# Input halves padded to 320 columns at one address modulo 256, and weight rings one buffer shorter, in an mLSTM and HGRN2 step

## The chip, the core and the metric

The kernel runs on one core of a Trainium2 chip. The metric is the device time of one execution in microseconds. A core has TensorE (PE, with the loading of weights shown apart as PEld), VectorE (DVE), ScalarE (ACT), GpSimd (POOL) and SyncE (SP, which issues the DMAs). Each engine works through its own rows in a fixed order and waits on semaphores for the others.

## What is computed

The reference is one step of a streaming encoder layer: 512 prompt columns of a new stream and 32 sample columns of a running one, D = 1024. In float32:

```python
xn = _rmsnorm(h, norm_g[l])
proj = xn @ w_in[l]
u, v_m, z_m, ig_pre, fg_pre, q_h, f_h, i_h, g_h, ga, gb = jnp.split(proj, _split_points(), axis=-1)
c, conv_new = _causal_conv(u, conv0[l].astype(u.dtype), conv_w[l], conv_b[l])
c = jax.nn.silu(c).astype(f32)
...
hm, C_new, n_new, m_new = _mlstm(qm, km, vm, ig, lf, C0[l].astype(f32), n0[l].astype(f32), m0[l].astype(f32))
hm = _head_layernorm(hm.transpose(0, 2, 1, 3), mnorm_g[l].astype(f32))
hm = (hm + m_skip[l].astype(f32) * c) * jax.nn.silu(z_m.astype(f32))
ya = hm.astype(x.dtype) @ w_brm[l]
...
oh, S_new = _hgrn(to_heads(qh), to_heads(kh), to_heads(i_h.astype(f32)), to_heads(lfh), S0[l].astype(f32))
oh = _head_rmsnorm(oh.transpose(0, 2, 1, 3), hnorm_g[l].astype(f32)) * jax.nn.silu(g_h.astype(f32))
yb = oh.astype(x.dtype) @ w_brh[l]
y = jax.nn.sigmoid(ga) * ya + jax.nn.sigmoid(gb) * yb
h = h + y @ w_out[l]
h = h + jax.nn.sigmoid(h @ w_pg[l]) * (p[l] @ w_ple[l])
```

`_mlstm` has 4 heads of width 512 (q and k are projections of the convolved u, with a causal convolution of width 4), `_hgrn` has 8 heads of width 128. The outputs are the normalised h and the new states.

## The kernel before

All activations lie with channels on the 128 partitions and the T = 544 columns (32 sample, 512 prompt) along the free axis; D is 8 such tiles. A matmul's output is one half, TH = 272 columns.

To keep float32 accuracy every projection is made of rounded parts: a value x is split into a high part (rounded to the matmul type, by ACT) and a low part (the rest, by DVE), and three matmuls add up high by high, high by low and low by high. The normalised input is kept for the whole kernel in `xs`: eight pairs `xh`, `xl` of 128x544 tiles (`norm`, `norm_low`, L1438 to 1447). Three functions read it as the moving operand: `dense` (L199; v of head 0, f = 1 to 3), `One` (L431; z of head 0) and `Two` (L549; all other projections). `Two` forms two output tiles out of seven products of half size instead of eight. A block is one product: 12 matmuls of 272 columns with one weight piece of 128x512. Its forms a11, a12 and s4 read a half of `xh`/`xl` (`moving`, L533), the forms s2, s3, s1 and a22 read one of the four slices of `xfh`/`xfl`, which are sums and differences of halves (`xf_sums`). The same class with another `xs` (the tiles `yh`, `yl`) makes `w_out`.

Weights pass through rings in SBUF, which all have buffers of 128 x 512 fp32:

- "wr": the raw piece, written by a DMA on SP (`raw_piece`), NRAW = 6 buffers
- "wh" and "wl": its high part, written by ACT, and its low part, by DVE (`split_piece` at L174 and L175, `high_piece`, `low_piece`), NPIECE = 6 buffers each
- "wu": sums of raw pieces for the forms s1 to s4 (`add`, L482), NSUM = 4 buffers

A buffer can be written again when the last row that reads it is done. For "wr" these readers are the split and the sums; for "wh" and "wl" they are PE's matmuls of the block.

What sets the order: PE's rows stand in an order written by hand throughout. ACT's and DVE's do so up to about 65 us and in the HGRN2 chain; in the heads of the mLSTM (about 50 to 650 us) and at the end, a scheduler places the rows when their inputs and buffers are free by its own estimate. `Pump` puts the blocks in order and calls for the splits AHEAD = 3 blocks ahead. Whatever order comes out is fixed in the program.

Other names that are spoken of: L904 and L906 copy transposed gate columns (`col`, `cols`) out of PSUM; `emc` (L1202, L1203) are small copies of them; L988 and L989 make high and low parts of q; L573 and L577 put projections of u into the convolution's input `ub`; L774 is a step of the convolution (`cv`); L1280 and L1282 scale y ahead of its transposes (L1290); L138 makes low parts of the merged head (`hm`); `wbm..` are weights of the merge `ya`.

## Time and profile before

| | |
|---|---|
| median of 3 runs | 1118.29 us (1117.81 to 1118.54) |
| span of the profiled execution | 1116.3 us |
| PE busy | 1108.7 us (99%), 8825 rows |
| DVE busy | 922.1 us (83%), 1969 rows |
| ACT busy | 714.8 us (64%), 1583 rows |
| granted TensorE clock | 1.00 in every stage |
| DMA, mean of the span | 122 GB/s |

The span is the time from the first to the last instruction of the execution that the profiler recorded; the time of a run has some more around it. A busy share counts time in which an engine works on at least one row; PE's matmuls overlap, so the time of a row (0.29 us for 272 columns) is longer than the pitch from one start to the next. Pitches are therefore taken from start times.

### The profile page before, as it was taken

What the parts mean: (1) busy time and instruction counts of PE and PEld (TensorE: products, weight loads), DVE (VectorE), ACT (ScalarE), POOL (GpSimd) and SP (SyncE); (2) the same over time, 40 slices, a digit from 0 to 9 for tenths busy, and PEclk for the clock granted to TensorE, in tenths of its full rate; (3) what the DMA queues carried; (4) which work ended last, traced back from release to release, by engine and by line L of the source; (5) the groups of instructions that cost most, each with busy time, mean ns of one, the idle gap of its engine ahead of it and who ended that gap; (6) DMA issues with size and microseconds to landing.
All of it is one profiled execution on the core that took longest, in us unless ns stands there. A gap on an engine that the chain in (4) does not pass through costs nothing.

```text
span 1116.3 us, 23756 instructions
## 1 busy us (share of the span) xinstructions
PE 1108.7 (99%) x8825; PEld 1097.3 (98%) x8825; DVE 922.1 (83%) x1969; ACT 714.8 (64%) x1583; POOL 158.4 (14%) x412
## 2 busy tenths in 40 slices
PE   9999999999999999999999999999999999999998
PEld 9999999999999999999999999999999999999998
DVE  6986998676896786986898699999999888789785
ACT  6686657754666555664667478787777776445662
POOL 5112021101010110101200123222322000000000
PEclk9999999999999999999999999999999999999999
DMA  6234225232264132461556322122222353333943
GB/s 224 77 95 128 86 67 176 96 114 96 74 215 157 39 124 104 131 222 53 195 176 206 107 77 83 56 84 74 84 75 74 109 166 114 111 125 103 304 150 119
DMA packets 78044, 135.78 MB, mean 122 GB/s; under 512 B 8804, under 2 KB 16612, under 8 KB 77928
## 3 DMA queue, kind: packets, MB, share of 16 engines
q1 hardware_dynamic: 77760, 134.21, 36.9%
q8 instruction: 69, 1.13, 0.4%
q14 instruction: 47, 0.39, 0.1%
q10 hardware_dynamic: 168, 0.06, 0.0%
HBM read 109.32 MB, written 24.91 MB: 120 GB/s over the span
## 4 chain that ended last, share of the span: by engine, by line
PE 94%; DVE 3%; ACT 1%; DMA 1%; issue 1%; SPq 0%; ACTq 0%; DVEq 0%
PE d L549 42%; PE ya L199 9%; PE pg L2017 4%; PE yb L199 4%; PE k L199 4%; PE q L199 4%; PE C L1069 3%; PE pl L1741 3%; PE u L326 2%; PE sc L1012 2%; PE v L199 2%; PE nm L1248 2%; PE d L431 1%; PE ple L199 1%; PE yt L1290 1%; PE ho L1855 1%
## 5 line engine op out<-in xcount | busy, mean ns | idle before, releaser
L566 ACT COPY t<-d 128x272 f32<-128x272 f32 x126 | 47.4, 376 | 5.2 <-PE d L549 5.0
L1762 DVE TENSOR_TENSOR hkq<-hkq,hq 128x288 f32<-128x288 f32 (+1 forms) x96 | 41.5, 439 | 5.6 <-PE pl L1741 2.5
L1696 ACT COPY km<-hkq 128x256 f32<-128x256 f32 x56 | 23.9, 427 | 30.5 <-DVE hkq L1762 28.4
L1741 PE MATMUL pl<-hkq,km 128*128 128x128 f32 x224 | 37.9, 291 | 0.6 <-ACT km L1696 0.6
L774 DVE SCALAR_TENSOR_TENSOR cv<-ub,vec,cv 128x547 f32<-128x547 f32 x48 | 37.0, 781 | 0.4
L1741 PEld LDWEIGHTS pl<-hkq,km 128*128 128x128 f32 x224 | 30.9, 190 | 2.7 <-ACT km L1696 1.6
L1177 DVE SCALAR_TENSOR_TENSOR c<-c,wi,Cs 128x258 f32<-128x258 f32 x32 | 15.1, 477 | 20.2 <-PE Cs L1175 20.1
L1081 ACT COPY Co<-C 128x258 f32<-128x258 f32 x30 | 9.8, 379 | 28.3 <-PE C L1069 20.7
L1316 DVE TENSOR_TENSOR y<-ya,y 128x272 f32<-128x272 f32 x48 | 18.8, 432 | 8.8 <-PE ya L199 8.7
L1776 DVE COPY_PREDICATED at<-lmask,pl 128x256 f32<-128x256 uint8 (+1 forms) x56 | 25.3, 452 | 0.3
L1259 ACT COPY y<-nm 128x516 f32<-128x516 f32 x16 | 9.4, 589 | 18.0 <-PE nm L1248 17.8
L1026 ACT CAST sh<-dm 128x512 fp32r<-128x512 f32 (+3 forms) x16 | 7.4, 459 | 20.4 <-DVE dm L1020 20.4
L939 POOL COPY vsm<-vt 128x96 f32<-128x96 f32 x16 | 7.2, 462 | 87.4 <-ACT vt L577 44.3
L1069 PE MATMUL C<-vh,kwh 128*128 128x258 f32 x96 | 19.3, 283 | 0.0
L1069 PE MATMUL C<-vh,kwl 128*128 128x258 f32 x96 | 19.3, 282 | 0.0
L1069 PE MATMUL C<-vl,kwh 128*128 128x258 f32 x96 | 19.3, 282 | 0.0
L1012 PE MATMUL sc<-q,kh 128*128 128x512 f32 (+3 forms) x80 | 18.6, 320 | 0.1
L1207 DVE BATCH_NORM_STATS2 bs<-y 128x6 f32<-128x512 f32 (+1 forms) x20 | 13.7, 687 | 5.1 <-ACT y L1259 5.0
L963 DVE TENSOR_TENSOR kl<-kf,kh 128x512 fp32r<-128x512 f32 x16 | 11.0, 686 | 8.1 <-ACT kh L962 8.0
L767 POOL COPY uo<-ub 128x3 f32<-128x3 f32 x16 | 7.6, 472 | 64.1 <-DVE ub L573 39.3
L1248 PE MATMUL nm<-vh,sh 128*128 128x258 f32 x80 | 16.5, 288 | 0.0
L1768 POOL TENSOR_TENSOR hq<-hq 128x136 f32<-128x136 f32 (+4 forms) x40 | 16.0, 399 | 3.1
(4666 smaller groups left out, 5119.2 us busy)
## 6 DMA issues: line engine op xcount, KB each, us to landing
ya_d<-y SPq DMA_DIRECT2D x32, 272.0 KB, 3.0
y<-ya_d SPq DMA_DIRECT2D x24, 272.0 KB, 3.8
c<-in_C SPq DMA_DIRECT2D x16, 258.0 KB, 4.5
out_Cs<-c SPq DMA_DIRECT2D x16, 258.0 KB, 2.8
out_Cp<-Co SPq DMA_DIRECT2D x15, 258.0 KB, 2.4
x<-in_xT SPq DMA_DIRECT2D x8, 272.5 KB, 4.7
ya<-ya_d SPq DMA_DIRECT2D x8, 272.0 KB, 4.8
h<-in_xT SPq DMA_DIRECT2D x8, 272.0 KB, 2.8
```

The source lines that it names most:

```text
L199: PE.matmul(both[b][:m, :TH], part(w, off + k * step, m, x), xx[:, half(b)], start=(k == 0 and j == 0), stop=(k == n - 1 and j == 2),)
L549: PE.matmul(ps, ww[:, c], xx, start=(start and k == 0 and j == 0), stop=end, skip_group_check=not start,)
L566: S.copy(t, ps)
L774: last = V.scalar_tensor_tensor(cv[:, :547], ub[:, j : j + 547], vcol(V_CW + 4 * ft + j), cv[:, :547], ALU.mult, ALU.add)
L1012: PE.matmul(pn[:, 0, :n], ks[f][x][:, j * P : (j + 1) * P], qs[f][y][:, NS + j * P : T], start=(f == 0 and i == 0), stop=(f == KH - 1 and ...
L1069: PE.matmul(pn[g][:, :VH], kw[b][x][:, f * P : (f + 1) * P], vv[b][y][:, g * VH : (g + 1) * VH], start=(b == 0 and j == 0), stop=(b == NB ...
L1248: PE.matmul(pn[:, g, :VH], st[j][x][:, (i - j) * P : (i - j + 1) * P], vv[j][y][:, g * VH : (g + 1) * VH], start=(j == 0 and q == 0), stop ...
L1696: S.copy(km.rearrange("p (n j c) -> p n j c", j=2, c=c), view(kk, HB, ((2 * c, NA // (2 * c)), (c - HB, 2), (1, c))),)
L1741: PE.matmul(pn[:, b * P : (b + 1) * P], km[:, b * P : (b + 1) * P], view(qq, b * P, ((2 * c, P // (2 * c)), (HB + c, 2), (1, c))), start=True,
L1762: V.tensor_tensor(x, x, t, ALU.mult)
L1776: V.copy_predicated(at[:, :n], lmask[:, li, :n], pn[:, :n])
L2017: PE.matmul(ps, part(w, k * P, P, x), xx[:, c], start=(k == 0 and j == 0), stop=(k == KD - 1 and j == 2))
```

## The change

Each tile of `xs` (and the tiles `yh`, `yl`) becomes 2 x 320 columns, of which each half uses the first 272. Two tiles that nothing uses (`gap`, 24 and 40 columns) move what follows them. All three piece rings lose a buffer: 16 tiles x 2 x 48 columns x 4 bytes are 6144 bytes a partition, as three buffers of 2048. Six small tiles have one buffer instead of two. `One` loses its parameter `cut`, which was always T/2 (TH).

```diff
+TW = 320
...
-NRAW = 6
+NRAW = 5
 NSUM = 4
-NPIECE = 6
+NPIECE = 5
...
+    gp = ctx.enter_context(tc.tile_pool(name="gp", bufs=1))
...
+    gp.tile([P, 24], F32, name="gap")
...
+    def xhalf(t, b):
+        return t[:, b * TW : b * TW + TH] if t.shape[-1] == 2 * TW else t[:, half(b)]
+
+    def xall(t):
+        return two(t)[:, :, :TH]
...
-                        xx[:, half(b)],
+                        xhalf(xx, b),
...
-        V.tensor_tensor(u, h1, l1, ALU.add)
+        V.tensor_tensor(two(u), xall(h1), xall(l1), ALU.add)
         for b, t in enumerate((x21, x22)):
-            V.tensor_tensor(t, h2[:, half(b)], l2[:, half(b)], ALU.add)
+            V.tensor_tensor(t, xhalf(h2, b), xhalf(l2, b), ALU.add)
...
-                        for b, c in enumerate(halves):
+                        for b in range(2):
                             PE.matmul(
-                                self.ps[b][:, : c.stop - c.start],
+                                self.ps[b][:, :TH],
                                 part(self.w, k * P, P, x),
-                                xx[:, c],
+                                xhalf(xx, b),
...
-                return tuple(x[:, b * TH : (b + 1) * TH] for x in self.xs[i * (KD // 2) + k])
+                return tuple(xhalf(x, b) for x in self.xs[i * (KD // 2) + k])
...
-            xh = cp.tile([P, T], F32R, name=f"xh{k}")
-            xl = cp.tile([P, T], F32R, name=f"xl{k}")
-            S.copy(xh, t[:, :T])
+            xh = cp.tile([P, 2 * TW], F32R, name=f"xh{k}")
+            xl = cp.tile([P, 2 * TW], F32R, name=f"xl{k}")
+            S.copy(xall(xh), two(t[:, :T]))
             xs.append((xh, xl))
...
-            V.tensor_tensor(xs[k][1], xt[k][:, :T], xs[k][0].bitcast(F32), ALU.subtract)
-
+            V.tensor_tensor(xall(xs[k][1]), two(xt[k][:, :T]), xall(xs[k][0].bitcast(F32)), ALU.subtract)
+
+        cp.tile([P, 40], F32, name="gap")
...
-            c = one if f == k else slice(0, T)
-            S.copy(yh[:, c], t[:, c])
-            V.tensor_tensor(yl[:, c], t[:, c], yh[:, c].bitcast(F32), ALU.subtract)
+            n = 1 if f == k else 2
+            yh, yl, tt = xall(yh)[:, :n], xall(yl)[:, :n], two(t[:, :T])[:, :n]
+            S.copy(yh, tt)
+            V.tensor_tensor(yl, tt, yh.bitcast(F32), ALU.subtract)
```

The number of rows on each engine and PE's order stay as they are. The scheduler's order of ACT and DVE differs in many places. Two of them are shown. A row gives the line, the operation, output from inputs and the shape; lines after the change are 8 or 9 higher.

DVE in q of head 0, before (`wq010l`, `wq011l` are low parts of q's weights for PE's next tile, `kl` and `q_` low parts of k and q):

```order
L963 TENSOR_TENSOR kl_1235<-kf_1200,kh_1234 128x512
L175 TENSOR_TENSOR wq010l<-wq01r_1391,wq010h 128x512
L175 TENSOR_TENSOR wq011l<-wq01r_1393,wq011h 128x512
L904 COPY col<-cols 128x72
L906 COPY cols<-cols 96x12
L989 TENSOR_TENSOR q_1330<-q_1305,q_1330 128x272
L989 TENSOR_TENSOR q_1330<-q_1304,q_1330 128x272
```

DVE at the same place after the change:

```order
L971 TENSOR_TENSOR kl_1240<-kf_1205,kh_1239 128x512
L912 COPY col<-cols 128x72
L914 COPY cols<-cols 96x12
L1210 COPY emc<-col 128x4 x2
L1211 COPY emc<-cols 32x1 x2
L997 TENSOR_TENSOR q_1303<-q_1277,q_1303 128x272
L997 TENSOR_TENSOR q_1335<-q_1310,q_1335 128x272
L997 TENSOR_TENSOR q_1335<-q_1309,q_1335 128x272
L184 TENSOR_TENSOR wq010l<-wq01r_1396,wq010h 128x512
L184 TENSOR_TENSOR wq011l<-wq01r_1398,wq011h 128x512
```

The two low parts of weights have moved behind the column copies, four `emc` copies and three low parts of q.

DVE in the projection of u of head 1, before (`wa..` and `ws..` are weight pieces of plain and summed forms; the L482 row is the sum that `ws310` is made from):

```order
L175 TENSOR_TENSOR wa1210l<-wi10r_4464,wa1210h 128x512
L482 TENSOR_TENSOR ws_4643<-wi10r_4371,wi11r_4373 128x512
L138 TENSOR_TENSOR hm7l<-c_2856,hm7h 128x544
L573 TENSOR_TENSOR ub_4385<-d_4384,t_4462 128x272
L175 TENSOR_TENSOR ws310l<-ws_4643,ws310h 128x512
L175 TENSOR_TENSOR ws110l<-ws_4576,ws110h 128x512
L573 TENSOR_TENSOR ub_4586<-d_4585,t_4604 128x32
L573 TENSOR_TENSOR ub_4586<-d_4585,t_4604 128x240
L774 SCALAR_TENSOR_TENSOR cv_4682<-ub_4385,vec,cv_4682 128x547
```

DVE at the same place after the change:

```order
L184 TENSOR_TENSOR wa1210l<-wi10r_4469,wa1210h 128x512
L147 TENSOR_TENSOR hm7l<-c_2861,hm7h 128x544
L490 TENSOR_TENSOR ws_4632<-ws_4583,wi10r_4469 128x512
L581 TENSOR_TENSOR ub_4390<-d_4389,t_4467 128x272
L490 TENSOR_TENSOR ws_4648<-wi10r_4376,wi11r_4378 128x512
L581 TENSOR_TENSOR ub_4591<-d_4590,t_4609 128x32
L581 TENSOR_TENSOR ub_4591<-d_4590,t_4609 128x240
L782 SCALAR_TENSOR_TENSOR cv_4687<-ub_4390,vec,cv_4687 128x547
L184 TENSOR_TENSOR ws310l<-ws_4648,ws310h 128x512
L184 TENSOR_TENSOR ws110l<-ws_4581,ws110h 128x512
```

The sum for `ws310` has moved behind the first `ub` row, and the low parts of `ws310` and `ws110` behind the second pair of `ub` rows and the convolution step. Head 2 has the same rows with other numbers.

## The prediction

> **What bounds the kernel now.** I read the busy shares first, then the chain that ended last, then the list of who waited for whom on PE, and then the order of time on PE and DVE around the places where the change moves rows.

> ```profile
> span 1116.3 us, 23756 instructions
> PE 1108.7 (99%) x8825; PEld 1097.3 (98%) x8825; DVE 922.1 (83%) x1969; ACT 714.8 (64%) x1583; POOL 158.4 (14%) x412
> PE 94%; DVE 3%; ACT 1%; DMA 1%; issue 1%; SPq 0%; ACTq 0%; DVEq 0%
> PE d L549 42%; PE ya L199 9%; PE pg L2017 4%; PE yb L199 4%; PE k L199 4%; PE q L199 4%; PE C L1069 3%; PE pl L1741 3%; PE u L326 2%; PE sc L1012 2%; PE v L199 2%; PE nm L1248 2%; PE d L431 1%; PE ple L199 1%; PE yt L1290 1%; PE ho L1855 1%
> ```

> PE is busy in 99% of the span and carries 94% of the chain, and 42% of the chain is one line, the matmuls of `Two` (L549). DVE at 83% and ACT at 64% have room on average. The longest total that the wait list gives for any line of PE is:

> ```profile
> PE warm L1386 <- DVE emc L1201: 1.1, 1, 1.1
> ```

> So PE hardly ever waits. Two things follow. Whatever changes the pitch of PE's matmuls counts in full. And any weight that DVE or ACT delivers later than PE wants it is a new wait that counts in full too, because there is no other wait that could swallow it. The change does one thing of each kind. The span is 1116.3 us and the median of the runs 1118.29, so about 2.0 us lie around the span; I add and subtract on the span and put these 2.0 us back. A measurement of this kernel can tell about 0.2% (2.2 us) from no change; so "same" is 1116.05 to 1120.53.

> **First part: the address of the moving operand.** A half of 272 fp32 columns is 1088 bytes, 64 more than a multiple of 256. By the program's allocations the halves of `xh` now start at 0 and 64 modulo 256 and those of `xl` at 128 and 192; with 320 columns and the two gap tiles all four start at 160. The four slices of `xfh`/`xfl` (sums of halves, also 272 columns) start at 160, 224, 32 and 96, and stay. So the trace of before already has matmuls with the moving operand at 160: the blocks of form s2 (weights `ws2..`). Here are starts of four blocks of 12 matmuls that follow each other without a break (columns: start, duration, engine, line, operation, output from inputs):

> ```profile
> 458.50 0.29 PE L549 MATMUL d<-xfh,wa2212h 128*128 128x272 f32 x1
> ...
> 460.02 0.29 PE L549 MATMUL d<-xfh,ws214h 128*128 128x272 f32 x1
> ...
> 461.50 0.29 PE L549 MATMUL d<-xh,ws412h 128*128 128x272 f32 x1
> ...
> 463.01 0.29 PE L549 MATMUL d<-xh,wa1214h 128*128 128x272 f32 x1
> ```

> The durations are alike, so they tell nothing; the pitch does. The block at 96 takes 460.02 - 458.50 = 1.52 us, the one at 160 takes 1.48, the first on `xh`/`xl` (64, 192) 1.51. Over the whole trace I averaged the pitch in all such blocks of 12: 33 at 160 give 123.8 ns a matmul, 129 blocks on `xh`/`xl` give 125.6, the other `xf` slices 125.5 (224), 126.3 (32) and 126.5 (96). The first and the last undisturbed block at 160:

> ```profile
> 231.15 0.29 PE L549 MATMUL d<-xfh,ws220h 128*128 128x272 f32 x1
> ...
> 232.50 0.29 PE L549 MATMUL d<-xfh,ws220l 128*128 128x272 f32 x1
> ...
> 936.86 0.29 PE L549 MATMUL d<-xfh,ws294h 128*128 128x272 f32 x1
> ...
> 938.22 0.29 PE L549 MATMUL d<-xfh,ws294l 128*128 128x272 f32 x1
> ...
> 938.34 0.29 PE L549 MATMUL d<-xh,ws486h 128*128 128x272 f32 x1
> ...
> 939.85 0.29 PE L549 MATMUL d<-xh,wa1294h 128*128 128x272 f32 x1
> ```

> Eleven pitches: 1.35 and 1.36 us, 123 to 124 ns each; the block on `xh`/`xl` right behind the last one takes 939.85 - 938.34 = 1.51, 126 ns each. The plain forms of L549 (1656 matmuls), z of head 0 at L431 (192) and three of the v tiles of head 0 at L199 (144) read `xh`/`xl`: 1992 matmuls move to 160. The block means price that at 1.8 ns x 1992 = 3.6 us; the mean of every 272-column matmul by its own address (124.2 at 160 against 125.3 to 126.2 at 0, 64, 128 and 192) prices it at about 1.4 x 1992 = 2.8. The address is not the only thing that differs between the blocks, so I take the middle, 1.6 ns: **-3.2 us**, bounds -2.7 and -3.6.

> [...]

> The same edit turns ACT's and DVE's writes of `xh`, `xl`, `yh`, `yl` and the sums from 128x544 into 2x272. The element count is the same:

> ```profile
> L1447 DVE TENSOR_TENSOR xl<-x,xh x8: 714/716/727, 35.2 to 43.3; 128x544 fp32r<-128x544 f32 x8
> ...
> 44.24 0.42 PE L199 MATMUL v<-xh,wv10h 128*128 128x272 f32 x2
> ```

> The eighth is done at 44.0. PE's projection of v reads the first tile from 44.2 and the eighth 42 matmuls, some 5 us, later: nothing; if a 2x272 row took twice as long, the eighth would come 5 us later and PE would wait a few tenths.

> **Second part: one buffer less in the rings.** Counts stay. What moves is order: a split of a weight piece can be placed only when a buffer of `wh` and `wl` is free, which is now one block of 12 later, and ACT and DVE run in a fixed order. Rows of DVE and ACT change at some 250 and 300 places. Mostly a piece had been ready 7 to 9 us ahead of PE and is now ready 6 us ahead: nothing. It matters where the piece falls behind something that itself waits; these are five places.

> Site A, q of head 0:

> ```profile
> 86.16 0.68 DVE L175 TENSOR_TENSOR wq010l<-wq01r,wq010h 128x512 fp32r<-128x512 f32 x1
> 87.89 0.52 PE L199 MATMUL q<-cs0h,wq010h 128*128 128x272 f32 x2
> 88.00 0.23 DVE L904 COPY col<-cols 128x72 f32<-128x72 f32 x1 [0.56 <-PE cols L902]
> 88.15 0.16 DVE L906 COPY cols<-cols 96x12 f32<-96x12 f32 x1
> 88.23 0.78 DVE L989 TENSOR_TENSOR q<-q,q 128x272 fp32r<-128x272 f32 x2
> 88.49 0.41 PE L199 MATMUL q<-cs0h,wq010l 128*128 128x272 f32 x2
> 90.29 0.16 DVE L1202 COPY emc<-col 128x4 f32<-128x4 f32 x1
> 90.36 0.14 DVE L1203 COPY emc<-cols 32x1 f32<-32x1 f32 x1
> ```

> Now `wq010l` is made at 86.16, ahead of the copy `col`, which waits for PE's transposes until 88.00. After the change DVE does `col` (0.15 from start to start), `cols` (0.08), four small copies `emc` (0.07 each), three low parts of q (0.39 each), and only then `wq010l` (0.68): 88.00 + 0.15 + 0.08 + 0.28 + 1.17 + 0.68 = 90.36. PE wants it at 88.49: **+1.9**. (ACT's high part, wanted at 87.89, is some 0.7 late too and lies inside the 1.9.) Behind `wq010l` stand `wq011l`, wanted 1.5 later and made 0.6 later, and the masks of the scores, whose broadcast is issued later by about as much as PE stalls.

> Sites B and C, where u of heads 1 and 2 is projected; B, at 315 us:

> ```profile
> 312.22 0.68 DVE L482 TENSOR_TENSOR ws<-wi10r,wi11r 128x512 f32<-128x512 f32 x1
> 313.74 0.44 DVE L573 TENSOR_TENSOR ub<-d,t 128x272 f32<-128x272 f32 x1 [0.20 <-PE d L549]
> 314.09 0.68 DVE L175 TENSOR_TENSOR ws310l<-ws,ws310h 128x512 fp32r<-128x512 f32 x1
> 314.90 0.29 PE L549 MATMUL d<-xh,wa1210l 128*128 128x272 f32 x1
> 315.28 0.29 PE L549 MATMUL d<-xfh,ws310l 128*128 128x272 f32 x1
> 315.30 0.50 DVE L573 TENSOR_TENSOR ub<-d,t 128x32 f32<-128x32 f32 x2
> 315.71 0.78 DVE L774 SCALAR_TENSOR_TENSOR cv<-ub,vec,cv 128x547 f32<-128x547 f32 x1
> ```

> Now `ws310l` is done at 314.77, half a us ahead of its matmul at 315.28. After the change the sum that it is made from (the `ws` add of 312.22) stands behind the `ub` of 313.74, and the low part stands behind the next `ub` pair and a convolution step. That `ub` pair reads the PSUM tile of `wa1210`, whose last matmul starts at 314.90, so it cannot begin before about 315.25: 315.25 + 0.41 + 0.70 + 0.68 = 317.04, against 315.28, and the signal: **+1.8**. The same rows stand 149.5 us later for head 2 (`ws314l` is read there where `ws310l` is here): **+1.8**. Behind `ws310l` the next low parts have 1.3 us or more in hand once PE has stalled.

> Site D, 585.8 us, transposes of y of head 3; site E, 170 to 174 us, end of u and first merge weights:

> ```profile
> 583.61 1.53 ACT L1280 ACTIVATE y<-y,mrs,rs 128x512 f32<-128x512 f32 x2
> 585.51 0.60 PE L1290 MATMUL yt<-ident,y 128*128 128x128 f32 x4
> ...
> 171.12 0.68 DVE L175 TENSOR_TENSOR wbm001l<-wbm00r,wbm001h 128x512 fp32r<-128x512 f32 x1
> 173.65 0.41 PE L199 MATMUL ya<-hm2h,wbm001l 128*128 128x272 f32 x2
> ```

> At D the two scalings on ACT (1.53 for both) now come behind `ws348h`, whose buffer comes free with the block that ends 12 matmuls ahead of the transposes, about 584.1 (585.51 less 12 x 0.125 and the signal): 584.1 + 0.55 + 1.53 = 586.2, where PE reads the second of them near 585.85: **+0.4**. At E `ws46l` slides behind `hm2l` (0.2 late) and `wbm001l` behind two convolution steps, to be done near 174.4 instead of 171.8, wanted at 173.85: **+0.7** in all. The sum is 1.9 + 1.8 + 1.8 + 0.4 + 0.7 = **+6.6 us**. Bounds: 5.0 if DVE gets through its queue quicker than the start-to-start times say, 8.5 with the small places that I left out (five of 0.1 to 0.4) and a late mask at A.

> The ring of raw pieces loses a buffer too, so its DMAs on SP are issued up to 3 us later. The latest of them:

> ```profile
> L482 DVE TENSOR_TENSOR ws<-wi25r,wi25r x1: 683/683/683, 350.9 to 350.9; 128x512 f32<-128x512 f32 x1
> ```

> There the piece would land about 3 us after DVE comes for it, so DVE would stand still that long, and with it kl and the splits behind it. PE reads the nearest of those more than 10 us later: I count nothing (bounds 0 and 3).

> **The sum.** 1116.3 - 3.2 + 6.6 = 1119.7 of span, 1121.7 with the 2.0 around it: slower by 3.4 us, 0.3%. The forecast with its bounds is 1118.7 to 1124.1 (-3.6 + 5.0 and -2.7 + 8.5).

> **The rivals.** (1) *The late weights are covered.* Place: A, B and C, which are 5.5 of the 6.6. With none of these the sum is -3.2 + 1.1 and the time 1116.2; with none of D and E either it is 1118.3 - 3.2 = 1115.1: faster. It decides at a stall sum of 1.0 us, from which the gain of 3.2 is over 0.2%. For it: DVE is only 83% busy, and PE now has no wait over 1.1 us, so whatever orders the work has done well so far. Against it: at A and B the piece stands behind a copy that waits for PE itself (0.56 and 0.20 of idle in the rows), so idle time elsewhere on DVE cannot help. (2) *Stalls and gain cancel.* If the waits at B and C are half of what the fixed chain of DVE says (0.9 each), because rows run closer together behind a wait than in the rows above, the stalls are 4.8 and the time 1119.9; with A halved too, 3.9 and 1119.0. For it: both terms are small and of opposite sign. (3) *The address does nothing by itself*: what makes the s2 blocks quick is their place in the order or their weights. Then the first term is 0 and the time 1116.3 + 6.6 + 2.0 = 1124.9. Against it: the 33 blocks at 160 are quick whatever head they stand in, and slices of the same tile at 32 and 96 are not. (4) *Raw pieces come late*: one stall of 3 us at one of three places like 350.9, giving 1124.7 or more.

> **Chances.** Forecast 0.58 (of which 0.07 falls below 1120.53); stalls and gain cancel 0.18; the weights are covered 0.13; the address does nothing 0.06; raw pieces late 0.05. Faster 0.13; same 0.18 + 0.07 = 0.25; slower 0.51 + 0.06 + 0.05 = 0.62. The range 1116.2 to 1125.0 takes in the forecast's bounds, the cancelling case and most of (3) and (4), and leaves out (1) and the tail above, some 0.18.

> **What would show it.** In the profile after: PE's wait list has entries of 1 to 2 us against DVE's low parts at 88.5, 315.3 and 465 us, and small ones near 174 and 585; blocks of 12 on `xh`/`xl` take 1.48 to 1.49 us like the s2 blocks do. If blocks stay at 1.51, the first term is wrong; if the wait list is as short as now, the second is; a wait on a DMA of a raw piece would be case (4). I would be most wrong if the low parts are made in time after all.

## The result, and the profile after

The changed kernel takes 1126.68 us (median of 4 runs, 1126.20 to 1128.72) against 1118.41 us (1117.81 to 1118.85): a ratio of 1.0079, 95% interval 1.0067 to 1.0091. It is slower by 8.3 us where 3.4 were forecast, and lies above the range. The profiled execution took 1126.99 us and has a span of 1125.3.

The top of the page of the kernel after (span; busy time of each engine; shares of the chain that ended last, by engine and by line):

```profile
span 1125.3 us, 23815 instructions
PE 1110.5 (99%) x8825; PEld 1095.5 (97%) x8825; DVE 921.3 (82%) x1969; ACT 715.2 (64%) x1583; POOL 157.4 (14%) x412
PE 83%; DVE 10%; DMA 3%; issue 2%; ACT 2%; SPq 0%; DVEq 0%; ACTq 0%
PE d L557 35%; PE ya L208 7%; PE q L208 4%; PE k L208 4%; PE pg L2027 4%; PE yb L208 4%; PE C L1077 3%; PE sc L1020 3%; PE u L335 2%; PE v L208 2%; PE pl L1750 2%; PE nm L1256 2%; PE d L439 2%; DVE hkq L1771 1%; DVE ws L515 1%
```

The busy shares look as before and would mislead. The chain of work that ended last doesn't: PE's part fell from 94% to 83%, DVE now carries 10% and DMA 3%. (The new helpers move the lines: L549 is now L557, L199 is L208, L175 is L184, L482 is L490.) What PE waited for, in the view of waits of the kernel after:

```profile
PE ya L208 <- DVE y L1324: 0.9, 1, 0.9
PE d L557 <- DVE ws314l L184: 0.7, 1, 0.7
PE d L557 <- DVE ws310l L184: 0.7, 1, 0.7
PE d L557 <- DVE vt L583: 0.7, 1, 0.7
PE q L208 <- DVE wq010l L184: 0.7, 1, 0.7
PE d L557 <- ACT ws310h L183: 0.7, 1, 0.7
PE d L557 <- ACT ws314h L183: 0.7, 1, 0.7
PE q L208 <- DVE q L997: 0.6, 1, 0.6
...
PE vts L1164 <- DVE vl L1156: 0.5, 1, 0.5
...
PE ya L208 <- DVE wbm001l L184: 0.4, 1, 0.4
```

Sites A (`wq010l`), B (`ws310l`) and C (`ws314l`) are there, each as a pair of waits, one for the high part or for q and one for the low part; E is `wbm001l`. The waits on `y` (at 625 us), `vt` (560) and `vl` (569) had no place in the forecast.

A wait's idle time is less than what it costs, because matmuls right behind it start further apart (0.23 us instead of 0.125 at site B below). So I matched PE's 8825 rows of the two traces, took start after less start before, and give below by how much that difference grew at each place. Times are those of the trace after.

| place | growth, us | forecast |
|---|---|---|
| A, 88 to 94 | 3.3 | 1.9 |
| E, 173 to 178 | 0.9 | 0.7 |
| B, 315 to 321 | 2.1 | 1.8 |
| C, 467 to 473 | 2.1 | 1.8 |
| D, 594 | 0.4 | 0.4 |
| 411 to 412, 560, 563 to 569, 625 | 2.7 | 0 |
| pitch on `xh`/`xl` | -3.7 | -3.2 |
| the rest, in places under 0.3 each | 0.9 | 0 |
| at the last matmul | 8.7 | 3.4 |

**Site A**, PE in order of time after (start, duration, engine, line, operation, output from inputs; idle before and its releaser in brackets), and two windows of 2 us in it (length; busy time of PE, PEld, DVE, ACT, POOL; granted clock; DMA share; GB/s):

```profile
88.84 0.39 PE L208 MATMUL q<-cs0h,wq010h 128*128 128x272 f32 x1 [0.65 <-DVE q L997]
...
90.15 0.82 PE L208 MATMUL q<-cs0h,wq010l 128*128 128x272 f32 x2 [0.67 <-DVE wq010l L184]
90.77 0.66 PE L208 MATMUL q<-cs1h,wq010h 128*128 128x272 f32 x2
91.22 0.66 PE L208 MATMUL q<-cs1l,wq010h 128*128 128x272 f32 x2
...
93.41 0.41 PE L208 MATMUL q<-cs3h,wq011h 128*128 128x272 f32 x2
93.65 0.42 PE L208 MATMUL q<-cs3l,wq011h 128*128 128x272 f32 x2
```

```profile
90.00:92.00 2.00, 1.85 (x8) 1.85 (x9) 1.97 (x10) 0.69 (x2) 1.51 (x5) 0.50 0.38 87
92.00:94.00 2.00, 2.00 (x13) 2.00 (x13) 0.11 (x2) 0.00 (x0) 0.00 (x0) 0.68 0.46 175
```

`wq010l` is read at 90.15 where it was 88.49, and counted with the matmul behind it the waits make 1.9 us, as forecast. But then pairs of matmuls start 0.45 us apart, 91.22 - 90.77, where two take 0.25 otherwise: 227 ns each, because the granted clock is 0.50. Some twelve matmuls run so, and at 93.65 - 93.41 = 0.24 it is over. That is another 1.3 to 1.4 us, at a clock that had been 1.00 in the same 8 us before:

```profile
88.00:96.00 8.00, 8.00 (x57) 7.66 (x58) 4.44 (x21) 6.59 (x21) 3.81 (x14) 1.00 0.38 117
```

**Site B**, all engines in order of time after:

```profile
317.54 0.68 DVE L490 TENSOR_TENSOR ws<-wi10r,wi11r 128x512 f32<-128x512 f32 x1
...
318.47 0.60 ACT L183 CAST ws310h<-ws 128x512 fp32r<-128x512 f32 x1
318.51 0.51 DVE L581 TENSOR_TENSOR ub<-d,t 128x32 f32<-128x32 f32 x2 [0.29 <-PE d L557]
318.93 0.78 DVE L782 SCALAR_TENSOR_TENSOR cv<-ub,vec,cv 128x547 f32<-128x547 f32 x1
319.12 0.39 PE L557 MATMUL d<-xfh,ws310h 128*128 128x272 f32 x1 [0.65 <-ACT ws310h L183]
...
319.63 0.68 DVE L184 TENSOR_TENSOR ws310l<-ws,ws310h 128x512 fp32r<-128x512 f32 x1
...
320.37 0.40 PE L557 MATMUL d<-xfh,ws310l 128*128 128x272 f32 x1 [0.73 <-DVE ws310l L184]
```

This is the queue that the prediction drew: the `ub` pair waits for PE, the convolution step follows it, and only then is `ws310l` made. PE waits 0.65 + 0.73 us here, and the matmul behind each wait starts about 0.23 us after the one before it instead of 0.125; the clock stays at 1.00.

**At 625 us**, DVE and PE after, where nothing had been forecast:

```profile
623.52 0.69 DVE L515 TENSOR_TENSOR ws<-wi64r,wi64r 128x512 f32<-128x512 f32 x1 [4.29 <-DMA wi64r<-in_w_in]
...
624.86 0.78 DVE L1324 TENSOR_TENSOR y<-ya,y 128x272 f32<-128x272 f32 x2
...
625.43 0.66 PE L208 MATMUL ya<-hm12h,wbm330h 128*128 128x272 f32 x2 [0.89 <-DVE y L1324]
```

The same sum of raw pieces before, on DVE:

```profile
609.99 0.69 DVE L507 TENSOR_TENSOR ws<-wi64r,wi64r 128x512 f32<-128x512 f32 x1 [1.30 <-DMA wi64r<-in_w_in]
```

DVE stands still 4.29 us for a raw piece where it stood 1.30. PE needs nothing made of that piece until much later. What it needs is the `y` row behind it, which empties the PSUM tile that the next `ya` is to write: PE loses 0.89 us of idle, 1.05 in starts.

**At 560 us** the row that PE waits for, `vt`, stands on DVE behind rows that wait for ACT, and ACT for the DMA of the old state `c`, not for a raw piece:

```profile
556.41 0.62 ACT L1139 CAST c0p<-c 128x516 fp32r<-128x516 f32 x1 [2.21 <-DMA c<-in_C]
557.07 0.70 DVE L1140 TENSOR_TENSOR c0p<-c,c0p 128x516 fp32r<-128x516 f32 x1 [1.87 <-ACT c0p L1139]
```

The second `c0p` of ACT waits 0.69 us more for that state. In the kernel before, the first waits 2.57 us and the second not at all.

**The pitch.** Starts of three blocks of 12 and of the one behind them, after:

```profile
945.89 0.28 PE L557 MATMUL d<-xfh,ws294h 128*128 128x272 f32 x1
...
947.37 0.29 PE L557 MATMUL d<-xh,ws486h 128*128 128x272 f32 x1
...
948.85 0.29 PE L557 MATMUL d<-xh,wa1294h 128*128 128x272 f32 x1
...
950.33 0.29 PE L557 MATMUL d<-xfh,ws394h 128*128 128x272 f32 x1
```

Each takes 1.48 us, those on `xh`/`xl` (the second and the third) as much as the one on `xfh`; the second took 1.51 before. The mean pitch of the 1992 matmuls on `xh`/`xl` (pitches of 150 ns and more, which are waits, left out) went from 125.58 to 123.69 ns, and the one on `xfh`/`xfl` stayed (125.59, 125.58). 1.89 ns x 1992 = 3.8 us; the differences of starts in the table add up to 3.7.

### The profile page after: what moved, and what is told of

It is laid out like the page before. It is cut to its first block, busy times and chain, and to the rows that moved or that the text cites. A ratio compares the mean times of both kernels' runs of the same rounds, so it can differ in the third digit from the quotient of the medians.

```text
span 1125.3 us, 23815 instructions
## 1 busy us (share of the span) xinstructions
PE 1110.5 (99%) x8825; PEld 1095.5 (97%) x8825; DVE 921.3 (82%) x1969; ACT 715.2 (64%) x1583; POOL 157.4 (14%) x412
## 4 chain that ended last, share of the span: by engine, by line
PE 83%; DVE 10%; DMA 3%; issue 2%; ACT 2%; SPq 0%; DVEq 0%; ACTq 0%
PE d L557 35%; PE ya L208 7%; PE q L208 4%; PE k L208 4%; PE pg L2027 4%; PE yb L208 4%; PE C L1077 3%; PE sc L1020 3%; PE u L335 2%; PE v L208 2%; PE pl L1750 2%; PE nm L1256 2%; PE d L439 2%; DVE hkq L1771 1%; DVE ws L515 1%
## 5 line engine op out<-in xcount | busy, mean ns | idle before, releaser
L965 ACT ACTIVATE kf<-k 128x272 f32<-128x272 f32 x32 | 11.0, 391 | 11.6 <-PE k L208 11.6
L947 POOL COPY ksm<-kf 128x96 f32<-128x96 f32 x16 | 8.0, 503 | 66.6 <-ACT kf L965 66.6
```

## The experiments

Each was run beside the kernel before on the same chip; the ratios are to that. rings_only, pieces_5, raw_5 and xs_at_96 share one chip, high_5, low_5, after_again and rings_again another, late_low and both_at_96 a third.

**rings_only**: the shorter rings, without the padding.

```diff
-NRAW = 6
+NRAW = 5
-NPIECE = 6
+NPIECE = 5
```

> The kernel before with both ring sizes at 5 and no padding; each engine has the rows of the changed kernel in the same order (two DVE rows apart). Theory 1 (the lost time is all from the shorter rings, and the address gives back 3.3): the stalls of the changed kernel stay, at 88, 174, 315, 465, 552, 585 and 616 us, and matmuls on xh/xl go back to 125.6 ns: 1126.7 + 3.3 = 1130.0 us. Theory 2 (padded tiles themselves slow something): 1118 to 1124 us.

Measured: 1126.61 us (1125.57 to 1129.20), ratio 1.0085 (1.0068 to 1.0102). The rings alone make the whole loss: the padding adds none. The time is 3.4 us below the 1130.0 that theory 1 gave, so the change of pitch did not count in full. In this profile the clock did not halve at A (1.00 from 88 to 96 us) and the wait at 625 us was 0.2.

**pieces_5** and **raw_5** split the rings; each is one line of the diff above (NPIECE alone, NRAW alone).

> The kernel before with only the rings of high and low parts at 5. Theory 1a (the five places of the prediction come from these rings; q of head 0 3.3, 170 to 174 us 0.9, heads 1 and 2 2.1 each, 585 us 0.4): 1118.4 + 8.8 = 1127.2 us, with no stall at 616 us. Theory 1b (the raw ring holds the splits up): under 1121 us.

> The kernel before with only the ring of raw pieces at 5. Theory 1a: only the places that the prediction did not have (406 us 0.5, 552 to 561 us 0.9, 616 us 1.3) stall: 1118.4 + 2.7 = 1121.1 us, and DVE waits some 4 us for wi64r near 616 us. Theory 1b: over 1124 us.

Measured: pieces_5 1126.85 us (1126.44 to 1128.22), ratio 1.0082 (1.0067 to 1.0097), with all the waits of A to E and the halved clock (0.79 from 88 to 96 us). raw_5 1119.91 us (10 runs, 1119.46 to 1121.07), ratio 1.0021 (1.0012 to 1.0030): +2.1, with none of A to E. Nothing was lost at 616 us either, although DVE stood still 3.0 us for `wi64r` there. PE's waits that grew, first as the kernel before has them in this view, then raw_5:

```profile
PE Cs L1175 <- DVE c L1177: 0.5, 2, 0.2
PE vt L1144 <- DVE vl L1148: 0.4, 1, 0.4
```

```profile
PE vt L1144 <- DVE vl L1148: 1.0, 2, 0.6
PE Cs L1175 <- DVE c L1177: 1.0, 3, 0.5
```

In starts the growth is 0.75 us at 408 us and 0.65 at 569, at rows that DVE makes late. The 0.65 at 569 is there in pieces_5 and high_5 too (0.67 and 0.68), where the raw ring has 6 buffers, so it comes with more than one order. Still, the raw ring alone is not free. But pieces_5 and rings_only, which differ by the raw ring, agree within their intervals: on top of the shorter "wh" and "wl" it adds nothing that these runs can tell.

**high_5** and **low_5** shorten only "wh" or only "wl"; each line stands at two places, and the other ring keeps 6.

```diff
-        hi = wp.tile([P, WP], F32R, tag="wh", name=name + "h")
+        hi = wp.tile([P, WP], F32R, tag="wh", name=name + "h", bufs=5)
...
```

```diff
-        lo = wp.tile([P, WP], F32R, tag="wl", name=name + "l")
+        lo = wp.tile([P, WP], F32R, tag="wl", name=name + "l", bufs=5)
...
```

> The kernel before with only the ring of high parts at 5; low parts and raw pieces keep 6. Theory: ACT's casts wait for a buffer of high parts and everything behind them slides, so nearly all of the 8.8 us of the shorter piece rings are here: 1125.5 to 1127 us, with PE's waits at 88, 174, 315, 465 and 585 us. Rival: the low parts, which stand on the busier engine, are the ones that hold: under 1122 us.

> The kernel before with only the ring of low parts at 5. Theory: 1120 to 1122 us, part of the wait at 88 us and small ones elsewhere, none over 0.5 us at 315 and 465 us. Rival: over 1125 us.

Measured: high_5 1125.85 us (1125.58 to 1127.82), ratio 1.0074 (1.0060 to 1.0087). PE's waits in it:

```profile
PE d L549 <- DVE ws310l L175: 0.8, 1, 0.8
PE q L199 <- DVE wq010l L175: 0.7, 1, 0.7
PE q L199 <- DVE q L989: 0.6, 1, 0.6
PE d L549 <- ACT ws310h L174: 0.6, 1, 0.6
```

These are the pairs of A and B (that of C, with `ws314`, is alike): a low part is late because its high part, from which it is made, has no buffer earlier. low_5 1123.10 us (1122.00 to 1124.02), ratio 1.0048 (1.0033 to 1.0063), more than expected, with waits at other rows:

```profile
PE q L199 <- DVE wq010l L175: 0.9, 1, 0.9
PE ya L199 <- DVE y L1316: 0.7, 1, 0.7
...
PE d L549 <- DVE ws214l L175: 0.2, 1, 0.2
```

In starts B and C lost 0.8 and 0.4 us of it. The costs of single rings don't add up: 7.8 and 5.0 alone, 9.1 together. Each ring length gives an order of its own, and each order has its own late rows.

**late_low**: the kernel before, rings of 6, but the weight `wq01` of head 0 (pieces `wq010` and `wq011`) is asked for only behind q's low parts. In the trace its high part stays early, and `wq010l` is made behind q's low parts, as in the order after, and behind five masks of the scores besides. This makes one wait at site A and none at B to E.

```diff
-        w = t.pop("wq", None) or weight(a["w_qm"][h, u], f"wq{h}{u}")
+        late = tc.issue_after(t["low"].ins) if (h, u) == (0, 1) else nullcontext()
+        with late:
+            w = t.pop("wq", None) or weight(a["w_qm"][h, u], f"wq{h}{u}")
...
+        t["low"], t["read"] = low, read
```

> The kernel before, all rings at 6, with one thing moved: the low parts wq010l and wq011l are issued behind q's low parts and the masks of the scores, as a single late piece at 88 us. PE should stand still once, for about 2.1 us. If that is all: 1118.0 + 2.1 = 1120.1 us. If a wait at this place also lets the clock drop to half for some 3 us, as in the changed kernel's profile (12 matmuls at 227 ns instead of 125): another 1.2 to 1.5, 1121.5 us.

Measured: 1122.30 us (5 runs, 1121.67 to 1123.59), ratio 1.0036 (1.0023 to 1.0049). PE in order of time, and the window of 2 us behind the wait:

```profile
90.67 0.52 PE L199 MATMUL q<-cs0h,wq010l 128*128 128x272 f32 x2 [2.06 <-DVE wq010l L175]
...
92.14 0.66 PE L199 MATMUL q<-cs2h,wq011h 128*128 128x272 f32 x2
92.59 0.66 PE L199 MATMUL q<-cs2l,wq011h 128*128 128x272 f32 x2
```

```profile
92.00:94.00 2.00, 2.00 (x11) 2.00 (x11) 0.00 (x0) 0.02 (x1) 0.00 (x0) 0.50 0.87 310
```

One late low part costs 2.1 us of waiting, and with the restart and some 15 matmuls at half clock 3.8 us by starts at A (3.3 in the changed kernel); 3.4 of it are left at the last matmul. So a late low part at this place, with all rings at 6, costs by itself what site A cost, though by one wait where the changed kernel has two.

**xs_at_96**: the changed kernel with its two gaps exchanged. The halves of `xs` then start at 96 instead of 160 modulo 256; weights (224) and order stay.

```diff
-    gp.tile([P, 24], F32, name="gap")
+    gp.tile([P, 40], F32, name="gap")
...
-        cp.tile([P, 40], F32, name="gap")
+        cp.tile([P, 24], F32, name="gap")
```

> The changed kernel with the gaps at 24 and 40 columns the other way round, so that the padded halves all start at 96 instead of 160 modulo 256, everything else at the same addresses and in the same order. If the address alone sets the pitch (126.5 ns for slices at 96 against 123.5): 1992 x 3.0 ns = 6.0, 1132.7 us. If it is only that the halves share one address: 1126.7 us. If the address does nothing and the gain has another source: 1126.7 us too, with the pitch at 123.5.

Measured: 1127.69 us (1127.22 to 1128.24), ratio 1.0087 (1.0072 to 1.0102). Starts of a block on `xh`/`xl` and of the next, as above:

```profile
947.63 0.29 PE L557 MATMUL d<-xh,ws486h 128*128 128x272 f32 x1
...
949.15 0.29 PE L557 MATMUL d<-xh,wa1294h 128*128 128x272 f32 x1
```

1.52 us instead of 1.48, 126.50 ns in the mean. An edit of nothing but addresses changes the pitch. The 1992 matmuls take 2.81 ns x 1992 = 5.6 us more, but the median moved by only 1.0 from the changed kernel's own (timed on another chip), 5.0 below the expected 1132.7. Most of this change of pitch did not reach the end. In the two profiles PE loses 2.5 us less here at 411, 560 and 625 us, behind waits that a DMA ends. That would fit: where PE comes later, it waits less for a transfer that lands when it lands. That this is the whole of it is not shown.

**after_again** and **rings_again**: the changed kernel and rings_only once more, in the same rounds, to see how much of the pitch's 3.7 us reaches the end.

> The changed kernel once more, on the same chip and in the same rounds as its counterpart without padding. If the address gain of 3.3 us that the pitches show reaches the end: 3.3 us (at least 2) below the counterpart. If it is given back at waits whose end PE's pitch does not set (pieces that come late by DMA, the clock after a stall): within 1 us of it. In the profile the pitch on xh/xl is 123.5 ns either way.

> The kernel before with both ring sizes at 5 and no padding, as the counterpart: 1126.6 us again by either theory; pitch on xh/xl 125.6 to 126 ns.

Measured: 1126.22 us (5 runs, 1124.97 to 1127.55), ratio 1.0073 (1.0061 to 1.0086), and 1128.49 us (1126.54 to 1128.78), ratio 1.0090 (1.0076 to 1.0104). They are 2.3 us apart in these rounds; over all runs the medians are 1126.4 (9 runs) and 1127.7 (8 runs), 1.4 apart. Pitches are 123.70 and 125.56 ns. So some 1.4 to 2.3 of the 3.7 us reach the end; the interval on that is as wide as the number.

**both_at_96**: the changed kernel with only the second gap shortened. `xs` starts at 96 and the weights at 160: both move down by 64 bytes.

```diff
-        cp.tile([P, 40], F32, name="gap")
+        cp.tile([P, 24], F32, name="gap")
```

> The changed kernel with the second gap 16 columns shorter, so that the padded halves move from 160 to 96 modulo 256 and everything behind them, the weights too (224 to 160), moves along by 64 bytes; order unchanged. If the place relative to the weights sets the pitch: 123.5 ns on xh/xl and 1126.4 us. If the address alone does: 126.5 ns and, with 1992 x 3.0 ns less what the noise of the waits hides, 1128 to 1132 us.

Measured: 1126.14 us (1125.70 to 1127.47), ratio 1.0072 (1.0056 to 1.0089), with a pitch of 123.67 ns, and 1.48 us for the same block:

```profile
946.68 0.29 PE L557 MATMUL d<-xh,ws486h 128*128 128x272 f32 x1
...
948.16 0.29 PE L557 MATMUL d<-xh,wa1294h 128*128 128x272 f32 x1
```

96 is slow beside weights at 224 (126.50 ns in xs_at_96) and quick beside weights at 160 (123.67). What decides is the place relative to what moved along, and of that these matmuls read only the weights: 64 bytes below them modulo 256 is quick. The slices of `xfh`/`xfl` bear it out: in the kernel before, those 64 below the weights (form s2) have 124.0 ns and those 128 below (form a22) 126.5.

## Why the prediction was right in sign and wrong in size

- **The bound was read rightly for late rows.** A row of PE that starts late is a loss, and no other wait swallowed it: the late weights reach the end nearly whole, in pieces_5 (9.1 us later at its last matmul, 9.1 in the median) as in late_low (3.8 made at A, 3.4 later at the last matmul, 4.2 in the median).
- **The term of the address (-3.2) was right as a pitch**: -3.7 by the trace, beside the upper bound of 3.6. Rival 3, that the address does nothing, fell: rings_only keeps 125.60 ns, xs_at_96 gets 126.50, the changed kernel 123.69. The reason given for the term was incomplete: both_at_96 shows that the distance to the weights counts (123.67 ns with the operand at 96 and the weights 64 above it).
- **"Whatever changes the pitch of PE's matmuls counts in full" is a step that failed.** Of the 3.7 us some 1.4 to 2.3 reach the end by the medians, and of the 5.6 us between the changed kernel and xs_at_96 only 1.0. The sum counted -3.2.
- **The term of the late weights (+6.6) was mis-sized, and that is the largest step that failed.** All five sites are where the prediction put them and for the reason that it gave, but for the first wait at A, which was for q's low parts and not for ACT's high part. They cost 8.8 us. I summed the delay of the weight and let PE go on at full pitch behind it. What was left out is the restart: the first matmul behind each wait comes about 0.1 us late (0.3 at A), and at A some twelve matmuls ran at half clock, which makes 1.3 to 1.4 us more. 8.8 lies beyond the bound of 8.5 too.
- **"I count nothing" for the ring of raw pieces failed too, and its size stays open.** I looked at one row, 350.9, and asked when PE needs what is made of that piece. In the profile after, PE lost 2.7 us at 411, 560 to 569 and 625 us, and there it waited not for a piece but for other rows of DVE: `vt`, `vl` and `y`, which PE needs or whose PSUM tile it needs at once. `vt` and `y` stood behind rows that waited, `vl` (569 us) behind splits of weights. At 625 us, and in part at 411 (0.75 us for `wi43r`), DVE's own wait was for a raw piece; at 560 us it came from the old state `c`. The same places lost 1.3 us in the second profile of the same kernel (after_again), 0.3 and 1.1 in rings_only and rings_again, and none in pieces_5. So 2.7 is what one execution had. raw_5 alone costs 2.1 us in the median of 10 runs. The upper bound of 3 held all of these; the value taken, 0, was at the wrong end.
- **Rivals 1 and 2** (weights covered; stalls and gain cancel) fell: no site was covered, and no wait was half of what the chain of DVE said. **Rival 4**, raw pieces late, was drawn as one case in 20 that takes the place of the forecast. At 625 us its mechanism came on top of the forecast, at another row.
- In the one profile the sum on the span is -3.7 + 8.8 + 2.7 = 7.8, and 0.9 stands in places under 0.3 that I did not follow up. By the medians the shorter "wh" and "wl" cost 9.1 us (pieces_5), the raw ring beside them -0.2 or 1.3 more (rings_only, rings_again, the second on another chip), and the padding gives back 1.4 to 2.3.
- The sum of the lower bound has a slip that changes nothing else: with -3.6 + 5.0 it is 1119.7, not 1118.7.

What stays open. The exact share of the pitch's gain that reaches the end: 1.4 to 2.3 of 3.7 us by the medians, with an interval as wide. Whether the raw ring adds anything beside shorter "wh" and "wl": alone it does, in company it can't be told. Where the rest of the pitch's gain goes is not shown place by place. A kernel with the padding and full rings was not tried: I found no other 6144 bytes to take.

## What to carry to other kernels

A buffer taken from a ring is priced by the order that it brings: list every row that slides behind another one, and for each engine ask what else stands behind the row that now waits, since it can be the unrelated row behind it (a PSUM tile to be emptied; 1.05 us of PE at 625 us here) that stops the busy engine. A late operand can cost more than its lateness (2.1 us of waiting made 3.8 by starts in late_low), so add the restart, about 0.1 us at a wait here, and look in the trace for a stretch at half clock, which at A made another 1.3 to 1.4 us. To use an address effect, change addresses alone first, weigh the measured pitch, 2 ns in 125 here, against what the bytes cost elsewhere, and don't count on all of it at the end.

## What the runs showed of the hardware

**The clock halved behind short waits at one place.** Site A's waits of 1.9 us in all (2.1 in late_low) come right behind some 1.3 us of transposes of 4 columns, and the granted clock fell to 0.50 for about 3.4 us: 0.79 in the mean of the 8 us from 88 to 96, and 8 x 0.21 / 0.50 = 3.4. It did so, with the same 0.79, in both profiles of the changed kernel and in those of pieces_5, xs_at_96, rings_again and late_low; not in those of rings_only and low_5 (1.00), which have waits there too (PE is idle for 1.31 and 1.05 us of the 8); and for twice as long, some 6.6 and 6.9 us by the same sum (0.59 and 0.57), in those of high_5 and both_at_96:

```profile
88.00:96.00 8.00, 6.71 (x29) 6.28 (x30) 4.49 (x20) 3.00 (x9) 3.62 (x8) 0.59 0.27 94
```

That is the window of high_5. At B and C, two waits of 0.7 us within 1.3 us between dense matmuls left it at 1.00 in the changed kernel (315 to 322 and 464 to 474 us). The same wait does or doesn't hit from run to run: one kernel has 1.31 us of idle there at 1.00 in rings_only and 1.32 at 0.79 in rings_again. What makes the clock fall, and how little work is enough for it, is not shown.

**One late transfer moved a stall by about a microsecond.** The wait at 625 us cost 1.05, 0.2, 0, 0.36 and 0.84 us of PE in five profiles (the changed kernel, rings_only, pieces_5, after_again, rings_again) of the same or nearly the same order of rows; DVE could read the raw piece behind it 3.2 us after its issue in the kernel before (609.99 - 606.78) and 5.7 in the changed one (623.52 - 617.78).
